# A hybrid attention and linear-recurrence layer on one core: four short gate scans, a PSUM copy shared by two engines, GpSimd's weight halves in quarters, and three memsets written earlier

## The chip, the core and the metric

The kernel runs on one core of a Trainium2 chip. The metric is the device time of one execution in microseconds (us). An instruction waits in its engine's queue behind every earlier instruction of that engine; the queues of different engines meet at semaphores.

## What is computed

One transformer layer over 16 learned meta rows and 1024 input rows of width 1024, all in float32. After an RMS norm, one projection feeds two groups of heads. Eight heads do "forgetting attention" (FoX) and four heads do a gated linear recurrence (HGRN2) in chunks; both results are joined, projected, added to the input, and followed by a SwiGLU feed-forward part. Cut to the two lines of the reference that the change touches:

```python
fox_log_f = jax.nn.log_sigmoid(ff + fox_f_bias)      # summed along the rows: s += c_i - c_j
S = jnp.exp(b_last)[..., None] * S + jnp.einsum('bhsk,bhsv->bhkv', k_dec, v_c)   # k_dec: decayed keys
```

## The kernel before

Nearly every matrix product is made of three matmuls: each float32 operand is split into a high part (a cast, on ScalarE) and a low part (source minus high part, on VectorE, or on GpSimd for some weights), and `mm3` (lines 170 to 173) issues high x high (L171), high x low (L172) and low x high (L173). These are called the dense matmuls below.

The program runs through five stages: norm, transposition and the recurrence's value projection (up to about 75 us of the trace); the HGRN heads 0 to 3 (to about 345 us); the FoX head pairs 0 to 3 (to about 575 us); the output projection; the feed-forward part (from about 675 us to the end). Stages are laid into one another: while the serial chain of one HGRN head runs on VectorE and ScalarE, TensorE fills its time with the dense matmuls of the next head's projection (`hgrn_proj`), and while attention of a pair runs, with the projection of the next pair (`fox_proj`).

Nobody writes this order out. The builder of the program takes the instructions in the order of the source, simulates them with costs of its own, and lets each engine's queue take what is ready first in that simulation. So a shorter instruction also moves other instructions, on other engines too.

What the change touches:

- `hgrn_compute` works in two units of 512 rows for each head, eight units in all. Near the end of a unit the decayed keys `kd` are transposed on TensorE (L486) into a PSUM bank, copied to `hE` by ScalarE (L488, called the key copy), and used as the stationary operand of four matmuls with the values (L491). Four VectorE instructions then update the state `S` (L498), four pairs of matmuls make the output (L495 and L496), and ScalarE and VectorE norm it before it is transposed again (L509).
- `fox_gates` sums the eight heads' gates along the rows. One scan (L349) runs over 1040 columns of 8 partitions; a mask `resetg`, written by GpSimd (L346, L348), starts the sum anew at three columns.
- `load_m` loads a 1024x128 weight. For the pairs 1 to 3, `fox_proj` has GpSimd make the low part (L140, 128x1024). There are two such weights for each pair, first for the keys and then for the queries.
- Ahead of the first pair's attention GpSimd clears two small tiles `mz` (L676) and the tail of the second head's value tile `v` (L545), in the source behind `fox_proj(0, ...)`. GpSimd also makes, for each head and each group of 256 queries, a swapped copy `QB` of the queries (L563, L564), the masked diagonal gates `dm` (L571) and a shift of the gates `nl` (L633). TensorE's score matmuls are L577 (with `QA`) and L578 (with `QB`), VectorE adds the gates to them (L583), and a score bank comes free when VectorE has read it.

Of the kernel before, what the change touches and what calls it, by code (L numbers as in the profile page):

```python
# [8 lines left out]
F32 = mybir.dt.float32  # L9
# [3 lines left out]
ALU = mybir.AluOpType  # L13
# [6 lines left out]
KT = D // P  # L20
META = 16
SEQ = 1024
L = META + SEQ
# [4 lines left out]
HEADS = 8  # L28
# [19 lines left out]
def f32(ap):  # L48
    return ap.bitcast(F32)
# [3 lines left out]
def hybrid_trunk(  # L53
# [18 lines left out]
    vec, act, pool, pe, sync = nc.vector, nc.scalar, nc.gpsimd, nc.tensor, nc.sync  # L72
# [65 lines left out]
    def split(hi, lo, src, engine=None):  # L138
        later(act.copy(hi, src))  # L139
        return later((engine or vec).tensor_sub(lo, src, f32(hi)))  # L140
# [17 lines left out]
    def load_m(c0, wsrc, engine=None):  # L158
        st = w1.tile([P, KT, P], F32, name="w_st", tag="w_st")
        sync.dma_start(out=st, in_=wsrc.rearrange("(k p) c -> p k c", p=P)[:, :, c0:c0 + P])  # L160
        hi = w1.tile([P, KT, P], F32R, name="w_hi", tag="w_hi")
        lo = w1.tile([P, KT, P], F32R, name="w_lo", tag="w_lo")
        split(hi, lo, st, engine)
        return hi, lo

    def after(ins, other):
# [164 lines left out]
    def fox_gates(z):  # L331
        az = fv.tile([P, NT + 1, HEADS], F32, name="az", bufs=1)
        act.activation(az, z, AF.Abs)
        act.activation(az, az, AF.Exp, scale=-1.0)
        act.activation(az, az, AF.Ln, bias=1.0)
        vec.tensor_scalar(z, z, 0.0, None, ALU.min)
        vec.tensor_sub(z, z, az)
        nlT = fv.tile([HEADS, L], F32, name="nlT", tag="wvh", bufs=1)
        for (dst, slots) in ((0, (NT,)), (META, (0, 1, 2, 3)), (META + 512, (4, 5, 6, 7))):
            pt = bank("tr")  # L340
            rows = META if slots[0] == NT else P
            for j, s in enumerate(slots):
                pe.transpose(pt[:HEADS, j * P:j * P + rows], z[:rows, s, :], ident[:rows, :rows])
            act.copy(nlT[:, dst:dst + rows * len(slots)], pt[:HEADS, :rows * len(slots)])
        resetg = fv.tile([HEADS, L], F32, name="resetg", tag="wvl", bufs=1)
        pool.memset(resetg, 1.0)  # L346
        for g in range(1, 4):
            pool.memset(resetg[:, META + 256 * g:META + 256 * g + 1], 0.0)  # L348
        vec.tensor_tensor_scan(nlT, resetg, nlT, 0.0, ALU.mult, ALU.add)  # L349
        sync.dma_start(out=nl_dram, in_=nlT)  # L350

    def hgrn_proj(h):
# [49 lines left out]
    def hgrn_compute(h, g, nk, qs, sgs, pm, kdm):  # L402
# [16 lines left out]
        for un in range(2):  # L419
# [65 lines left out]
            for c in range(4):  # L485
                pe.transpose(pt[:, c * P:(c + 1) * P], kd[:, c * P:(c + 1) * P], ident)  # L486
            kdT = hg.tile([P, 512], F32, name="hE", tag="hE")
            act.copy(kdT, pt)  # L488
            sb = bank("tr")
            for c in range(4):  # L490
                pe.matmul(sb[:, c * P:(c + 1) * P], lhsT=kdT[:, c * P:(c + 1) * P], rhs=hv[:, 4 * un + c, :], start=True, stop=True)  # L491
# [49 lines left out]
    def v_load(p, j, pool_):  # L541
        h = 2 * p + j
        vt = pool_.tile([P, NT + 1, P], F32R, name=f"v{j}", tag=f"v{j}", bufs=1)
        sync.dma_start(out=f32(vt[:, :NT, :]), in_=v_dram[:NT, :, h, :].rearrange("t p c -> p t c"))
        pool.memset(f32(vt[:, NT, :]), 0.0)  # L545
        for r0 in (0, 32):
            sync.dma_start(out=f32(vt[r0:r0 + META, NT, :]), in_=v_dram[NT, :META, h, :])
        return vt
# [118 lines left out]
    fx0_pool = left("fx0")  # L667
    fx0 = fx0_pool.__enter__()
    vs0, gts0 = {0: v_load(0, 0, fx0)}, [gate_load(0, j, fx0) for j in range(2)]
    b = fox_proj(0, fxk0)  # L670
    hg_pool.__exit__(None, None, None)
    fx_pool, fxk1_pool = right("fx", 2), right("fxk1")
    fx, fxk1 = fx_pool.__enter__(), fxk1_pool.__enter__()
    mzs = [fx.tile([P, 256], F32R, name=f"mz{i}", bufs=1) for i in range(2)]
    for t in mzs:
        pool.memset(f32(t), 0.0)  # L676
    for s in range(3):
        fox_compute(s, *b, *((vs0, gts0) if s == 0 else ()))
        if s == 0:
            fx0_pool.__exit__(None, None, None)  # L680
        b = fox_proj(s + 1, (fxk0, fxk1)[(s + 1) % 2])
# [522 lines left out]
```

## Time and profile before

| | us |
|---|---|
| median of 3 runs | 1296.89 (1296.81 to 1297.6) |
| the profiled execution, its own time | 1297.19 |
| span of its trace | 1295.2 |
| TensorE busy in the span | 1263.7 |
| VectorE, ScalarE, GpSimd busy | 908.6, 620.8, 126.4 |

A row of a timeline is one instruction, or several merged: start, busy time, engine, line, what it writes and reads, shapes, count; in brackets the idle time of the engine just before it and what ended it. Neighbouring instructions of one engine overlap at their ends, so the distance of two starts tells what one costs.

### The profile page before, as it was taken

The page shows a single profiled execution, that of the slowest core. Times are in us where ns is not written, and L with a number is a line of the kernel's source. Part 1 is how long each engine was busy: PE and PEld are TensorE (multiplying, and loading weights), DVE is VectorE, ACT ScalarE, POOL GpSimd, SP SyncE. Part 2 cuts the span into 40 slices and gives each one's busy share as a digit, 9 for nine tenths or more (in the row PEclk, how much of TensorE's full clock was granted, in tenths as well). Part 3 has the DMA queues.
Part 4 walks back from the last instruction along what each step waited for, and adds up shares of the span by engine and source line. Part 5 has one row for each costly group of instructions (what it writes and reads, how often), then busy time and mean ns, then how long its engine had stood idle before and what let it go on. Part 6 is the DMA issues. An engine that isn't in the chain of part 4 may idle for free.

```text
span 1295.2 us, 18497 instructions
## 1 busy us (share of the span) xinstructions
PE 1263.7 (98%) x6553; PEld 1066.5 (82%) x6553; DVE 908.6 (70%) x1889; ACT 620.8 (48%) x1334; POOL 126.4 (10%) x260
## 2 busy tenths in 40 slices
PE   8999999999899999899999999999999999999997
PEld 6888898988788888778868888888888888888886
DVE  6467666575597877796788766666666664697777
ACT  6356656464567666664453333233323333443364
POOL 1220101010334342210000000000000000000000
PEclk8999999999999999999999999999999999999999
DMA  7231212123222121533314323333332337854452
GB/s 255 74 115 45 73 42 74 58 60 115 66 92 63 59 63 47 180 111 116 127 49 139 123 82 121 122 111 106 118 122 74 114 122 265 305 194 147 122 170 82
DMA packets 135196, 146.37 MB, mean 113 GB/s; under 512 B 6984, under 2 KB 95368, under 8 KB 135104
## 3 DMA queue, kind: packets, MB, share of 16 engines
q1 hardware_dynamic: 135104, 145.19, 34.4%
q8 instruction: 52, 0.85, 0.3%
q14 instruction: 40, 0.33, 0.1%
HBM read 105.98 MB, written 39.19 MB: 112 GB/s over the span
## 4 chain that ended last, share of the span: by engine, by line
PE 81%; DVE 9%; ACT 4%; issue 2%; DMA 2%; POOL 1%; SPq 0%; DVEq 0%; ACTq 0%; POOLq 0%
PE pb L171 10%; PE pb L173 10%; PE pb L172 10%; PE dense L173 8%; PE dense L171 8%; PE dense L172 8%; PE g L171 4%; PE g L172 4%; PE g L173 4%; PE o L618 3%; PE tr L608 2%; PE g L577 1%; PE g L578 1%; DMA w_st<-in_w_in_dram 1%; PE o L172 1%
## 5 line engine op out<-in xcount | busy, mean ns | idle before, releaser
L172 PE MATMUL dense<-u_lo,w_hi 128*128 128x512 f32 (+2 forms) x384 | 141.0, 367 | 0.0
L171 PE MATMUL dense<-u_hi,w_hi 128*128 128x512 f32 (+2 forms) x384 | 140.2, 365 | 0.0
L173 PE MATMUL dense<-u_hi,w_lo 128*128 128x512 f32 (+2 forms) x384 | 139.5, 363 | 0.0
L172 PE MATMUL pb<-T_lo,bh 128*128 128x512 f32 x352 | 137.3, 390 | 0.3 <-DVE T_lo L140 0.2
L173 PE MATMUL pb<-T_hi,bl 128*128 128x512 f32 x352 | 136.9, 389 | 0.1
L171 PE MATMUL pb<-T_hi,bh 128*128 128x512 f32 x352 | 136.8, 390 | 0.2 <-ACT bh L139 0.2
L139 ACT CAST bh<-sS 128x512 fp32r<-128x512 f32 x88 | 54.3, 621 | 150.2 <-DVE sS L846 69.3
L139 ACT CAST h_hi<-h_st 128x1024 fp32r<-128x1024 f32 (+1 forms) x43 | 41.8, 972 | 82.3 <-PE o L172 37.8
L172 PEld LDWEIGHTS pb<-T_lo,bh 128*128 128x128 f32 x352 | 66.1, 188 | 15.0 <-DVE T_lo L140 1.2
L171 PEld LDWEIGHTS pb<-T_hi,bh 128*128 128x128 f32 x352 | 66.0, 188 | 14.4 <-ACT bh L139 0.6
L173 PEld LDWEIGHTS dense<-u_hi,w_lo 128*128 128x128 f32 x384 | 72.5, 189 | 6.2
L173 PEld LDWEIGHTS pb<-T_hi,bl 128*128 128x128 f32 x352 | 66.1, 188 | 14.0 <-DVE bl L140 0.4
L172 PEld LDWEIGHTS dense<-u_lo,w_hi 128*128 128x128 f32 x384 | 72.8, 190 | 5.8
L171 PEld LDWEIGHTS dense<-u_hi,w_hi 128*128 128x128 f32 x384 | 72.8, 190 | 5.7
L171 PE MATMUL pb<-w_hi,h_hi 128*128 128x512 f32 x198 | 77.0, 389 | 0.0
L172 PE MATMUL pb<-w_lo,h_hi 128*128 128x512 f32 x198 | 77.0, 389 | 0.0
L173 PE MATMUL pb<-w_hi,h_lo 128*128 128x512 f32 x198 | 77.0, 389 | 0.0
L140 DVE TENSOR_TENSOR w_lo<-w_st,w_hi 128x1024 fp32r<-128x1024 f32 (+1 forms) x41 | 49.8, 1214 | 36.8 <-ACT w_hi L139 36.6
L140 DVE TENSOR_TENSOR h_lo<-h_st,h_hi 128x1024 fp32r<-128x1024 f32 (+1 forms) x43 | 48.3, 1123 | 29.2 <-ACT h_hi L139 28.6
L139 ACT CAST w_hi<-w_st 128x1024 fp32r<-128x1024 f32 (+1 forms) x47 | 48.9, 1041 | 40.0 <-PE dense L172 17.3
L171 PE MATMUL g<-B_hi,w_hi 128*128 128x512 f32 x168 | 65.7, 391 | 0.8 <-ACT p L874 0.7
L172 PE MATMUL g<-B_lo,w_hi 128*128 128x512 f32 x168 | 65.4, 389 | 0.0
(861 smaller groups left out, 3344.1 us busy)
## 6 DMA issues: line engine op xcount, KB each, us to landing
w_st<-in_w_in_dram SPq DMA_DIRECT2D x24, 512.0 KB, 4.0
w_st<-in_w_ffn_gate_dram SPq DMA_DIRECT2D x22, 512.0 KB, 3.7
w_st<-in_w_ffn_up_dram SPq DMA_DIRECT2D x22, 512.0 KB, 3.9
B<-in_w_ffn_down_dram SPq DMA_DIRECT2D x20, 512.0 KB, 6.1
h_st<-S SPq DMA_DIRECT2D x20, 512.0 KB, 3.8
h_st<-A SPq DMA_DIRECT2D x15, 512.0 KB, 4.3
A<-g SPq DMA_DIRECT2D x22, 256.0 KB, 2.0
S<-u SPq DMA_DIRECT2D x22, 256.0 KB, 2.9
```

Source lines behind the costliest of these rows:

```text
L139: later(act.copy(hi, src))
L140: return later((engine or vec).tensor_sub(lo, src, f32(hi)))
L171: pe.matmul(o, lhsT=ah, rhs=bh, start=first, stop=False, skip_group_check=skip)
L172: pe.matmul(o, lhsT=ah, rhs=bl, start=False, stop=False, skip_group_check=skip)
L173: pe.matmul(o, lhsT=al, rhs=bh, start=False, stop=last, skip_group_check=skip)
L577: pe.matmul(sc[:, :w], lhsT=QA[:, P * i:P * (i + 1)], rhs=KS[:, c0:c0 + w], start=True, stop=False)
L578: pe.matmul(sc[:, :w], lhsT=QB[:, P * ii:P * (ii + 1)], rhs=KS[:, c0:c0 + w], start=False, stop=True)
L608: pe.transpose(pt[:, o + ii * P:o + (ii + 1) * P], Ss[ii][:, c:c + P], ident)
L618: m = pe.matmul(ob[:, q0:256], lhsT=vt[:, blk, :], rhs=r[:, q0:256], start=blk == NT, stop=blk == 2 * g + 1 and i == 3)
```

## The change

The one scan becomes four, over 272, 256, 256 and 256 columns, that read a constant 1.0 broadcast along the row; `resetg` and its memsets are gone. Of the key copy ScalarE keeps the first 256 columns and VectorE copies the other 256. GpSimd makes a weight's low part in four instructions of 128x256. The memsets of `mz` and of the second head's value tile (with that tile's load) stand ahead of `fox_proj(0, ...)` in the source.

```diff
-        split(hi, lo, st, engine)
+        if engine is None:
+            split(hi, lo, st)
+            return hi, lo
+        act.copy(hi, st)
+        for k in range(0, KT, 2):
+            engine.tensor_sub(lo[:, k:k + 2], st[:, k:k + 2], f32(hi[:, k:k + 2]))
...
-        resetg = fv.tile([HEADS, L], F32, name="resetg", tag="wvl", bufs=1)
-        pool.memset(resetg, 1.0)
-        for g in range(1, 4):
-            pool.memset(resetg[:, META + 256 * g:META + 256 * g + 1], 0.0)
-        vec.tensor_tensor_scan(nlT, resetg, nlT, 0.0, ALU.mult, ALU.add)
+        for a, b in ((0, META + 256), (META + 256, META + 512), (META + 512, META + 768), (META + 768, L)):
+            vec.tensor_tensor_scan(nlT[:, a:b], reset4[:HEADS, 1:2].to_broadcast([HEADS, b - a]), nlT[:, a:b], 0.0, ALU.mult, ALU.add)
...
-            act.copy(kdT, pt)
+            act.copy(kdT[:, :256], pt[:, :256])
+            vec.tensor_copy(kdT[:, 256:], pt[:, 256:])
...
-    b = fox_proj(0, fxk0)
...
         pool.memset(f32(t), 0.0)
+    vs0[1] = v_load(0, 1, fx)
+    b = fox_proj(0, fxk0)
```

Lines of the changed kernel stand 2 to 5 further down than before: L486 is L488 there, L491 is L494, L495 and L496 are L498 and L499, the low parts of GpSimd are L168, the dense matmuls L176 to L178.

TensorE's queue in the first unit, from the transposition of the decayed keys (`tr` out of `ident` and `hX`) to the first output matmuls, before:

```order
L486 MATMUL tr<-ident,hX 128x128 x4
L448 MATMUL g<-hX 128x128 x2
L172 MATMUL dense<-u_lo,w_hi 128x384
L173 MATMUL dense<-u_hi,w_lo 128x384
L171 MATMUL dense<-u_hi,w_hi 128x384
L491 MATMUL tr<-hv,hE 128x128 x4
L495 MATMUL o<-hv,AT 128x128
L496 MATMUL o<-S,hY 128x128
```

The same place after the change:

```order
L488 MATMUL tr<-ident,hX 128x128 x4
L450 MATMUL g<-hX 128x128 x2
L177 MATMUL dense<-u_lo,w_hi 128x384
L494 MATMUL tr<-hv,hE 128x128 x2
L498 MATMUL o<-hv,AT 128x128
L494 MATMUL tr<-hv,hE 128x128 x2
L499 MATMUL o<-S,hY 128x128
L498 MATMUL o<-hv,AT 128x128
```

Two dense matmuls that stood ahead of the four value matmuls now stand behind them, and the four are two pairs with an output matmul between.

TensorE's queue in the last unit, from the last dense matmuls of the first pair's keys (384 wide) on; `g` out of `KS` and `QA` is a score matmul of the first pair, and the 512-wide dense matmuls are that pair's second query projection, 24 in all. Before:

```order
L173 MATMUL dense<-u_hi,w_lo 128x384
L171 MATMUL dense<-u_hi,w_hi 128x512
L448 MATMUL g<-hX 128x128 x2
L491 MATMUL tr<-hv,hE 128x128 x4
L577 MATMUL g<-KS,QA 128x256
L172 MATMUL dense<-u_lo,w_hi 128x512
L173 MATMUL dense<-u_hi,w_lo 128x512
L495 MATMUL o<-hv,AT 128x128
```

After:

```order
L176 MATMUL dense<-u_hi,w_hi 128x384
L177 MATMUL dense<-u_lo,w_hi 128x384
L450 MATMUL g<-hX 128x128 x2
L494 MATMUL tr<-hv,hE 128x128 x2
L580 MATMUL g<-KS,QA 128x256
L494 MATMUL tr<-hv,hE 128x128 x2
L498 MATMUL o<-hv,AT 128x128
L499 MATMUL o<-S,hY 128x128
```

The three 512-wide matmuls of this piece have moved behind the output matmuls. Further on, 14 of the 24 stand behind the unit's first output transposition (L509, now L512) where 9 stood before, and three 272-wide dense matmuls stand behind the first two matmuls that read `QB`, where all 24 of their kind stood ahead of them.

GpSimd's queue from the low parts of the second pair's two weights (`w_lo`) to the first pair's gates (`nl`), with the numbers of the buffers. Before:

```order
L140 TENSOR_TENSOR w_lo_4411<-w_st_4408,w_hi_4410 128x1024
L140 TENSOR_TENSOR w_lo_4417<-w_st_4414,w_hi_4416 128x1024
L676 MEMSET mz0_3661 128x256
L676 MEMSET mz1_3662 128x256
L545 MEMSET v1_3665 128x128
L563 COPY QB_3672<-QA0_3580 64x256
L564 COPY QB_3672<-QA0_3580 64x256
L571 AFFINE_SELECT dm_3676<-nl0_3572 128x128
```

After (the first line is the whole first weight and the second three quarters of the second):

```order
L168 TENSOR_TENSOR w_lo_4417<-w_st_4414,w_hi_4416 128x256 x4
L168 TENSOR_TENSOR w_lo_4426<-w_st_4423,w_hi_4425 128x256 x3
L678 MEMSET mz0_3593 128x256
L678 MEMSET mz1_3594 128x256
L548 MEMSET v1_3597 128x128
L566 COPY QB_3678<-QA0_3602 64x256
L567 COPY QB_3678<-QA0_3602 64x256
...
L168 TENSOR_TENSOR w_lo_4426<-w_st_4423,w_hi_4425 128x256
L548 MEMSET v0_4490 128x128
L636 TENSOR_SCALAR nl0_3578<-nl0_3578,tg0_3580 128x272
L574 AFFINE_SELECT dm_3733<-nl1_3582 128x128
```

The memsets keep their place behind the weights; one quarter has moved behind the first six `QB` copies, ahead of the gates. At the next two pairs both weights are done, as before, ahead of one `dm` and the `QB` copies that follow it.

## Rows read from the trace of the kernel before

**Rows 1.** The page: busy us, share of the span and instructions of each engine.

```profile
PE 1263.7 (98%) x6553; PEld 1066.5 (82%) x6553; DVE 908.6 (70%) x1889; ACT 620.8 (48%) x1334; POOL 126.4 (10%) x260
```

**Rows 2.** The waits of TensorE, summed by who waited for whom: us in total, times, longest.

```profile
PE tr L491 <- ACT hE L488: 2.5, 8, 0.4
PE g L578 <- POOL QB L564: 2.0, 1, 2.0
...
PE g L577 <- DVE rr L590: 1.0, 1, 1.0
```

**Rows 3.** The timeline of TensorE and VectorE in the first unit.

```profile
114.02 1.16 PE L491 MATMUL tr<-hv,hE 128*128 128x128 f32 x8 [0.34 <-ACT hE L488]
...
115.22 1.64 DVE L498 SCALAR_TENSOR_TENSOR S<-S,hP,tr 128x128 f32<-128x128 f32 x4 [1.22 <-PE tr L491]
```

**Rows 4.** The timeline of ScalarE and VectorE in the second unit, and TensorE's wait behind it.

```profile
135.09 0.59 ACT L488 COPY hE<-tr 128x512 f32<-128x512 f32 x1
...
135.09 0.69 DVE L482 TENSOR_TENSOR hY<-hP,hg_q 128x512 f32<-128x512 f32 x1 [0.96 <-ACT hP L480]
...
136.92 1.64 DVE L498 SCALAR_TENSOR_TENSOR S<-S,hP,tr 128x128 f32<-128x128 f32 x4
138.59 1.22 DVE L425 TENSOR_TENSOR_SCAN hP<-reset,hg_g 128x512 f32<-128x512 f32 x1
...
142.25 0.33 PE L509 MATMUL tr<-ident,hE 128*128 128x128 f32 x1 [0.55 <-ACT hE L506]
```

**Rows 5.** The timeline around the gate scan: a 256-wide cast out of PSUM by ScalarE, a 256-wide read of PSUM by VectorE, the scan and what follows it on VectorE.

```profile
302.64 0.37 ACT L326 CAST vt<-dense 128x256 fp32r<-128x256 f32 x1 [3.21 <-DMA v_dram<-vt]
...
303.05 0.42 DVE L327 TENSOR_TENSOR vt<-dense,vt 128x256 fp32r<-128x256 f32 x1 [3.08 <-ACT vt L326]
...
309.69 2.31 DVE L349 TENSOR_TENSOR_SCAN nlT<-resetg,nlT 8x1040 f32<-8x1040 f32 x1 [0.66 <-ACT nlT L344]
311.93 0.39 DVE L472 TENSOR_TENSOR hP<-hP 128x256 f32<-128x256 f32 x1
```

**Rows 6.** TensorE in the last two units: its waits, and the first and the last of the nine 512-wide dense matmuls behind the first L509.

```profile
313.56 0.33 PE L486 MATMUL tr<-ident,hX 128*128 128x128 f32 x1 [0.98 <-ACT hX L400]
...
335.02 0.33 PE L486 MATMUL tr<-ident,hX 128*128 128x128 f32 x1 [0.22 <-ACT hX L400]
...
337.46 1.16 PE L491 MATMUL tr<-hv,hE 128*128 128x128 f32 x8 [0.38 <-ACT hE L488]
...
344.15 0.33 PE L509 MATMUL tr<-ident,hE 128*128 128x128 f32 x1 [0.26 <-ACT hE L506]
344.24 0.48 PE L171 MATMUL dense<-u_hi,w_hi 128*128 128x512 f32 x1
...
346.33 0.39 PE L172 MATMUL dense<-u_lo,w_hi 128*128 128x512 f32 x1
346.56 0.39 PE L173 MATMUL dense<-u_hi,w_lo 128*128 128x512 f32 x1
```

**Rows 7.** From the second weight's high part (ScalarE) through GpSimd's queue to the two waits of TensorE and the one of VectorE.

```profile
346.76 1.05 ACT L139 CAST w_hi<-w_st 128x1024 fp32r<-128x1024 f32 x1 [1.88 <-PE dense L172]
...
347.88 2.39 POOL L140 TENSOR_TENSOR w_lo<-w_st,w_hi 128x1024 fp32r<-128x1024 f32 x1 [6.71 <-ACT w_hi L139]
350.21 0.57 POOL L676 MEMSET mz<- 128x256 f32 x2
...
350.99 0.39 POOL L563 CAST QB<-QA 64x256 fp32r<-64x256 f32 x1
...
354.96 0.54 POOL L571 TENSOR_SCALAR_AFFINE_SELECT dm<-nl 128x128 f32<-128x128 f32 x2
...
351.89 0.51 PE L578 MATMUL g<-KS,QB 128*128 128x256 f32 x2 [1.98 <-POOL QB L564]
...
355.79 0.42 PE L577 MATMUL g<-KS,QA 128*128 128x400 f32 x1 [0.96 <-DVE rr L590]
...
355.28 0.35 DVE L583 CUSTOM_DVE_ANT_0 S__3731<-g,dm,mx 128x128 f32<-128x128 f32 x1 [1.26 <-POOL dm L571]
```

**Rows 8.** GpSimd's groups, shapes kept apart: busy us and mean ns of one instruction.

```profile
L633 POOL TENSOR_SCALAR nl<-nl,tg 128x784 f32<-128x784 f32 x8 | 7.8, 974 | 2.2 <-DVE mx L583 1.9
...
L633 POOL TENSOR_SCALAR nl<-nl,tg 128x272 f32<-128x272 f32 x8 | 3.9, 492 | 10.1 <-DVE mx L583 7.3 <-issue 2.7
```

**Rows 9.** The next pair's second weight, the `QB` copy behind it, and the first score matmul that reads a fresh `QB` there.

```profile
409.81 2.39 POOL L140 TENSOR_TENSOR w_lo<-w_st,w_hi 128x1024 fp32r<-128x1024 f32 x1 [6.42 <-ACT w_hi L139]
...
412.51 0.39 POOL L564 CAST QB<-QA 64x256 fp32r<-64x256 f32 x1
...
414.65 0.34 PE L578 MATMUL g<-KS,QB 128*128 128x384 f32 x1
```

**Rows 10.** Stretches of 2 us: length, busy time and count of TensorE, its weight loads, VectorE, ScalarE and GpSimd, granted clock, share and rate of the DMA engines.

```profile
350.00:352.00 2.00, 0.11 (x1) 0.11 (x2) 0.36 (x1) 0.32 (x1) 1.80 (x7) 1.00 0.01 3
...
522.00:524.00 2.00, 0.49 (x2) 0.30 (x2) 1.97 (x6) 1.95 (x4) 1.21 (x2) 1.00 1.08 291
524.00:526.00 2.00, 1.25 (x4) 0.90 (x5) 1.94 (x3) 1.60 (x4) 0.96 (x2) 0.82 1.00 218
526.00:528.00 2.00, 2.00 (x6) 1.54 (x5) 1.53 (x6) 0.00 (x0) 0.26 (x1) 0.50 0.92 336
528.00:530.00 2.00, 2.00 (x10) 1.78 (x10) 1.32 (x7) 0.00 (x0) 0.97 (x3) 0.83 0.98 381
```

## The prediction

> **What bounds the kernel now.** I read the page's busy times first, then TensorE's waits summed by who was waited for, then the timelines around every line that the change touches, and last GpSimd's groups and 2 us stretches with the granted clock. TensorE is busy 1263.7 of 1295.2 us [rows 1], so 31.5 us of idle time is all that can be won without taking matmuls away, and the change takes none away. Of that idle time it can reach three pieces: the eight waits of L491 for the key copy, 2.5 us in all; the first wait for a `QB`, 2.0; and a wait of 1.0 behind VectorE that is really GpSimd's `dm` [rows 2]. The last two are one place, 347 to 356, where GpSimd's queue is the path. So the question in each part is whether a shorter or longer step ends a wait of TensorE, or whether another step is late just behind it.
>
> **The key copy in halves.** In the first unit L491 waits 0.34 for the copy, and its eight matmuls end at 115.18, where VectorE's state update L498 starts after a wait of 1.22 [rows 3]. ScalarE's copy of 512 columns takes 0.59 [rows 4]; a 256-wide cast out of PSUM took 0.37, and a 256-wide VectorE read of PSUM 0.42 [rows 5]. So both halves, side by side, end 0.22 earlier at best, and eight units give 8 x 0.22 = 1.8 us as the largest gain. VectorE's own busy time grows by 8 x 0.42 = 3.4 us.
>
> What is late next: in the first unit two 384-wide dense matmuls, which filled the time of the copy, now stand behind L491. A 512-wide one costs 0.23, the distance of two starts [rows 6], so 384 columns cost 0.17 each, and the wait becomes 0.34 - 0.22 + 2 x 0.17 = 0.46. The two matmuls are not lost, they are done later. But L498 needs all four value products, and the second pair now stands behind an output matmul of about 0.22: 0.58 + 0.22 + 0.58 = 1.38 in the place of 1.16 [rows 3]. The group starts 0.22 earlier and lasts 0.22 longer, so `S` comes at the same time. In the second unit VectorE's queue is full from L498 through the scan L425, and TensorE waits 0.55 at L509 for what comes out of it [rows 4]; an earlier copy makes that wait longer by what it saves. VectorE's 0.42 lies in its own wait for the transposition's products, idle anyway before L498 (1.22 in the first unit). If that cover is gone, the units whose end is set by VectorE's chain pay it: three times 0.42 = +1.3. I take 0, between -1.8 and +1.3, because the two units that I followed both give back what they win.
>
> **Four scans.** A scan over 512 columns takes 1.22 [rows 4], over 1040 columns 2.31 [rows 5]: 1.09 for 528 columns, 2.06 ns each, and 0.16 fixed. Four over the same 1040 columns are 2.14 + 4 x 0.16 = 2.80, +0.49; bounds 0 (the fixed part overlaps) and +0.5. It lies on a path: VectorE goes from the scan straight to the chain of the seventh unit (L472, 311.93) [rows 5], behind which TensorE waits 0.98 at 313.56 [rows 6]. That wait grows by 0.49. What comes later and isn't fed by it gives some back: the waits of 0.22 at 335.02 and 0.38 at 337.46 [rows 6] shrink when TensorE comes later to them. I let +0.2 through to the end of the last unit and count it there. The mask's memsets on GpSimd are on no path, and their going is worth 0.
>
> [...]
>
> **The last unit and GpSimd's queue.** Here the order matters more than the durations. In the last unit two of the three 512-wide matmuls of the listed piece no longer stand between L491 and the first output matmuls: -0.46. With the copy's -0.22 and the +0.2 from the scans the unit's first L509 (344.15) comes about 0.45 to 0.5 earlier. Nine 512-wide dense matmuls stood behind it, the last at 346.56 [rows 6]; now there are 14, 5 x 0.23 = 1.15 more. The next weight's high part on ScalarE (346.76) starts when the last but one of these has ended, and GpSimd's low part (347.88, 2.39 us) when the high part has [rows 7]. So both start 0.65 to 0.7 later.
>
> Then the quarters. A quarter is not in the trace. The low end is 2.39 / 4 = 0.60. GpSimd's `nl` gives the fixed part: 0.974 for 784 columns and 0.492 for 272 [rows 8], 0.94 ns for each and 0.24 fixed; the whole weight bears that once and a quarter as well, so a quarter is (2.39 - 0.24) / 4 + 0.24 = 0.78, the high end. I take 0.75, near the high end, because `nl` is the nearest row of the same engine and a similar size. Three quarters are then 2.25, 0.14 less than the whole. The fourth no longer stands ahead of the first `QB` copies but ahead of `dm`.
>
> [...]
>
> So the first `QB` comes 0.65 - 0.14 = 0.5 later, and TensorE's wait at 351.89 grows by about that. Three 272-wide dense matmuls (3 x 0.12 = 0.37) that TensorE did ahead of this wait it now does behind it, in the next wait, at no cost. `dm` (354.96) comes 0.5 + 0.75 = 1.25 later; VectorE waits 1.26 for it at L583 (355.28) and TensorE behind that at L577 (355.79) [rows 7]. The delay at the end of this place is the later of the two, not their sum: **+1.25**. Bounds: +0.45 (the scans cost nothing, a quarter takes 0.60), and +1.7 (the scans' 0.49 goes through whole, a quarter takes 0.78).
>
> **Pairs 2 and 3.** Both weights still stand ahead of one `dm` and the `QB` copies there, so these come 4 x 0.75 - 2.39 = 0.6 later. The copy at 412.51 is one of two of 0.39; both would be done by 413.3, and its first reader stands at 414.65 without a wait [rows 9]: 1.3 us of slack hide the 0.6. I take +0.1 for each of the two places, for readers that are nearer than the one shown, +0.2; bounds 0 and +1.4 (0.6 and what queues behind it).
>
> **The moved memsets** keep their place in GpSimd's queue behind the weights, where they take 0.78, from 350.21 to the `QB` copy at 350.99 [rows 7], and win nothing: 0.
>
> **Sum.** 0 + 1.25 + 0.2 = +1.45 on the profiled execution's 1297.19 is 1298.64; that execution is 0.30 above the median of the runs shown, so 1298.3.
>
> **The rivals.** *Faster.* [...] 0.10.
>
> *Slower by a clock fall.* [...] 0.18.
>
> *Nothing changes.* The halves win 0.22 in some units (together about -1.2), GpSimd's place loses about that, and the moved memsets do nothing, since the queue keeps them: 1296.9 to 1297.2. For it: terms of both signs and similar size. Against it: the key copy's waits are short of followers in few units only. 0.22.
>
> **How the numbers follow.** My forecast, the sum, gets 0.50. About 0.2% (2.6 us) is what a measurement of this kernel can tell from no change: 1294.3 to 1299.5. The forecast lies inside it, with a tail above it where the key copy's +1.3 or the pairs' +1.4 comes: 0.07 of its 0.50. So slower is 0.18 + 0.07 = 0.25, faster 0.10, and the same 0.43 + 0.22 = 0.65. The range goes from 1295.2, the sum with the low ends of the key copy and of GpSimd's place (1298.3 - 1.8 - 0.8 = 1295.7) and 0.5 towards the faster rival, to 1300.6, the clock rival with the pairs' excess; it leaves out the faster rival and the sum of all high ends.
>
> **What would show it.** Right: L491's waits fall to about half, and L498 starts no earlier; a quarter takes 0.70 to 0.78; the four scans together 2.7 to 2.8; the first wait for `QB` is 2.4 to 2.6 and the wait for `dm` behind it over 1.5; the granted clock at 350 stays 1.00. Wrong: TensorE's idle time falls by over 1 us in the HGRN stage, or a quarter takes 0.60, or the second wait at 355 doesn't grow though `dm` is later, or the clock at 350 or at 524 is another than before.

## The result, and the profile after

| | before | after |
|---|---|---|
| median, lowest, highest of 18 runs each, us | 1296.16 (1294.38 to 1297.81) | 1298.82 (1297.01 to 1299.90) |
| the profiled execution, its own time | 1297.19 | 1299.88 |
| span of its trace | 1295.2 | 1298.2 |

The ratio is 1.0018 (95% interval 1.0012 to 1.0025): the changed kernel is slower by 2.7 us in the medians, 1.6 to 3.2 by the interval. The forecast was 1298.3, +1.4 on its own base. The time lies in the range and the sign is right, but the loss is nearly twice the sum, and most of it stands in another place.

TensorE's row on the page, and its waits summed by who was waited for (us, times, longest), which answer to [rows 1, 2]:

```profile
PE 1263.3 (97%) x6553; PEld 1066.1 (82%) x6553; DVE 913.1 (70%) x1900; ACT 620.2 (48%) x1334; POOL 125.7 (10%) x274
```

```profile
PE tr L512 <- ACT hE L509: 2.6, 4, 0.9
...
PE g L581 <- POOL QB L567: 2.1, 1, 2.1
PE tr L494 <- ACT hE L490: 1.7, 5, 0.5
...
PE o L499 <- DVE S L501: 1.0, 4, 0.3
```

The reader is to see that the waits for the key copy fell, from 2.5 us in eight to 1.7 in five, and that two others have come up in their place. TensorE now waits 1.0 us in four at the output matmuls that read the state S, where the list of the kernel before has no wait. At the output transposition (L512) it waits 2.6 us in four, where the kernel before waited twice, 0.55 and 0.26 [rows 4, 6]. TensorE has as much work as before, 1263.3 against 1263.7 [rows 1].

Where the time went can be read from the starts of a few TensorE instructions that both kernels issue. The first four are the state products of the heads 0 to 3 (L415, `tr` out of `kdmT`, one at the start of each head), then the first key transposition of the seventh unit (L486), the first matmul that reads a `QB`, the first 400-wide score matmul, and the 272-wide score matmul behind the wait at 523. Between them lie the heads 0, 1 and 2, the end of the gate scan, the last two units with GpSimd's place, and the pairs 0 to 2. The numbers in the first two rows are the distances of these starts. The last two units lie in the column "to the first QB", together with GpSimd's weights.

| us | head 0 | head 1 | head 2 | to unit 7 | to the first QB | to the 400-wide | pairs 0 to 2 |
|---|---|---|---|---|---|---|---|
| before: starts 104.93, 170.34, 237.84, 309.91, 313.56, 351.89, 355.79, 522.81 | 65.41 | 67.50 | 72.07 | 3.65 | 38.33 | 3.90 | 167.02 |
| after: 104.96, 170.77, 239.07, 311.94, 315.19, 353.84, 358.44, 525.80 | 65.81 | 68.30 | 72.87 | 3.25 | 38.65 | 4.60 | 167.36 |
| after less before | +0.40 | +0.80 | +0.80 | -0.40 | +0.32 | +0.70 | +0.34 |

So +2.0 of the +2.96 arises in the heads 0 to 2, where only the key copy differs and TensorE does the same matmuls. The next three columns do not hold the same matmuls in both kernels: one dense matmul of 512 columns (0.23 us) has moved out of "to unit 7", and three of 272 columns (0.37) have moved into "to the 400-wide". Only their sum compares like with like: from the scans to the end of GpSimd's place the change costs -0.40 + 0.32 + 0.70 = +0.62.

**The key copy.** VectorE's timeline in the fourth unit (the second of head 1) of the kernel before; this place is in no group:

```profile
198.10 1.22 DVE L140 TENSOR_TENSOR w_lo<-w_st,w_hi 128x1024 fp32r<-128x1024 f32 x1
199.24 1.22 DVE L425 TENSOR_TENSOR_SCAN hP<-reset,hg_g 128x512 f32<-128x512 f32 x1
200.40 0.35 DVE L498 SCALAR_TENSOR_TENSOR S<-S,hP,tr 128x128 f32<-128x128 f32 x1
...
203.12 0.34 DVE L498 SCALAR_TENSOR_TENSOR S<-S,hP,tr 128x128 f32<-128x128 f32 x1
```

The same unit after the change, VectorE, ScalarE and TensorE (L490 and L491 are the two halves of the copy, L494 the value matmuls):

```profile
198.59 1.22 DVE L140 TENSOR_TENSOR w_lo<-w_st,w_hi 128x1024 fp32r<-128x1024 f32 x1
199.06 0.37 ACT L490 COPY hE<-tr 128x256 f32<-128x256 f32 x1
199.73 0.42 DVE L491 COPY hE<-tr 128x256 f32<-128x256 f32 x1
200.87 0.62 DVE L371 SCALAR_TENSOR_TENSOR hg_n<-gx,lnomlb,gs 128x384 f32<-128x384 f32 x1 [0.72 <-ACT gs L367]
...
201.94 0.35 DVE L501 SCALAR_TENSOR_TENSOR S<-S,hP,tr 128x128 f32<-128x128 f32 x1
...
203.12 1.21 DVE L427 TENSOR_TENSOR_SCAN hP<-reset,hg_g 128x512 f32<-128x512 f32 x1
...
205.09 0.34 DVE L501 SCALAR_TENSOR_TENSOR S<-S,hP,tr 128x128 f32<-128x128 f32 x1
```

```profile
199.49 0.71 PE L494 MATMUL tr<-hv,hE 128*128 128x128 f32 x4 [0.32 <-ACT hE L490]
...
200.74 0.48 PE L178 MATMUL dense<-u_hi,w_lo 128*128 128x512 f32 x1
201.06 0.40 PE L176 MATMUL dense<-u_hi,w_hi 128*128 128x512 f32 x1
201.29 0.61 PE L494 MATMUL tr<-hv,hE 128*128 128x128 f32 x4
...
209.34 0.33 PE L512 MATMUL tr<-ident,hE 128*128 128x128 f32 x1 [0.57 <-ACT hE L509]
```

ScalarE's half starts at 199.06 and takes 0.37, as forecast. VectorE's half takes the forecast 0.42, but it starts 0.67 later, behind the low part `w_lo` of the next head's weight (198.59, 1.22 us). Not all of the 0.67 is the low part's: in each of the eight units VectorE's half starts only after ScalarE's has ended, 0.40 to 0.73 behind its start, and in the first and the seventh VectorE is idle before it, 0.23 and 0.59, until ScalarE's half is done. TensorE's own queue then adds to it: two dense matmuls stand ahead of the second pair of value matmuls, which start 1.1 us after the half is there (201.29 against 200.15). The builder's simulation, it seems, had the half later still; that is not shown. A scan of 1.2 us stands between the state updates as well. The first S starts 201.94 against 200.40, the last 205.09 against 203.12. Seen from the unit's first key transposition (196.66 before, 197.14 after) that is 1.06 and 1.49 us later, and TensorE waits 0.57 at the output transposition, where the view of the kernel before shows no wait in this unit.

The second unit, which the prediction followed, loses too (changed kernel; the rows before are in [rows 4]):

```profile
136.72 0.61 PE L494 MATMUL tr<-hv,hE 128*128 128x128 f32 x4
137.37 1.63 DVE L501 SCALAR_TENSOR_TENSOR S<-S,hP,tr 128x128 f32<-128x128 f32 x4 [0.50 <-PE tr L494]
...
142.70 0.33 PE L512 MATMUL tr<-ident,hE 128*128 128x128 f32 x1 [0.55 <-ACT hE L509]
```

Counted from the unit's first key transposition (133.42 before, 133.57 after), the first S starts 0.30 later, behind the second pair of value matmuls, and the output transposition 0.29 later, with the same wait of 0.55.

**The scans.** One merged row, which answers to the scan in [rows 5]:

```profile
311.18 2.46 DVE L351 TENSOR_TENSOR_SCAN nlT<-reset,nlT 8x272 f32<-8x272 f32 x4
```

The four take 2.46 together, 0.15 more than the one. And the view shows no wait ahead of them: the one scan had waited 0.66 for ScalarE to bring the last columns [rows 5], while the first of the four starts at 311.18, 0.44 before ScalarE's last copies into that tile end (311.62).

**GpSimd's place.** The rows that answer to [rows 7, 8]: GpSimd's queue, the two waits of TensorE, VectorE's wait for the gates, and the group of all quarters (busy us, mean ns):

```profile
350.11 2.12 POOL L168 TENSOR_TENSOR w_lo<-w_st,w_hi 128x256 fp32r<-128x256 f32 x3 [5.07 <-ACT w_hi L166]
...
356.30 0.73 POOL L168 TENSOR_TENSOR w_lo<-w_st,w_hi 128x256 fp32r<-128x256 f32 x1
...
353.84 0.51 PE L581 MATMUL g<-KS,QB 128*128 128x256 f32 x2 [2.07 <-POOL QB L567]
...
358.44 0.42 PE L580 MATMUL g<-KS,QA 128*128 128x400 f32 x1 [1.29 <-DVE rr L593]
...
357.94 0.35 DVE L586 CUSTOM_DVE_ANT_0 S__3737<-g,dm,mx 128x128 f32<-128x128 f32 x1 [1.60 <-POOL dm L574]
```

```profile
L168 POOL TENSOR_TENSOR w_lo<-w_st,w_hi 128x256 fp32r<-128x256 f32 x24 | 17.1, 737 | 56.1 <-PE dense L178 35.2 <-ACT w_hi L166 20.8
```

GpSimd's first low part, the norm's first and third step on VectorE in the last unit, and TensorE's wait behind them, after; the last row is the first of these steps before:

```profile
342.19 2.85 POOL L168 TENSOR_TENSOR w_lo<-w_st,w_hi 128x256 fp32r<-128x256 f32 x4 [35.23 <-PE dense L178]
342.96 0.69 DVE L108 TENSOR_SCALAR rs_v<-oss 128x4 f32<-128x4 f32 x1 [1.36 <-ACT hE L506]
344.47 0.59 DVE L112 TENSOR_TENSOR rs_t<-rs_t,rs_v 128x4 f32<-128x4 f32 x1
345.91 0.33 PE L512 MATMUL tr<-ident,hE 128*128 128x128 f32 x1 [0.91 <-ACT hE L509]
...
342.26 0.17 DVE L108 TENSOR_SCALAR rs_v<-oss 128x4 f32<-128x4 f32 x1 [1.30 <-ACT hE L503]
```

The two steps, 128x4 each, take 0.69 and 0.59 where they took 0.17 and 0.16 before, and each ends 0.02 us after a quarter on GpSimd (343.63 and 345.04). Whether the quarters hold them up was not tested.

The granted clock around GpSimd's place and around the later fall, in stretches of 2 us with the columns of [rows 10]:

```profile
352.00:354.00 2.00, 0.16 (x1) 0.16 (x2) 0.59 (x1) 0.00 (x0) 1.80 (x7) 1.00 0.01 3
...
356.00:358.00 2.00, 1.15 (x10) 0.76 (x8) 0.24 (x3) 0.45 (x2) 1.91 (x6) 1.00 0.51 152
526.00:528.00 2.00, 0.66 (x4) 0.27 (x3) 1.97 (x4) 1.95 (x5) 1.88 (x3) 0.85 1.08 290
528.00:530.00 2.00, 2.00 (x6) 1.49 (x5) 1.94 (x5) 0.70 (x2) 0.02 (x1) 0.50 0.76 233
530.00:532.00 2.00, 2.00 (x9) 1.68 (x8) 1.14 (x6) 0.00 (x0) 0.70 (x1) 0.79 0.80 307
```

### The profile page after: what moved, and what is told of

Its sections match the earlier page's. It is cut to its first block, busy times and chain, and to the rows that moved or that the text cites. A ratio compares the mean times of both kernels' runs of the same rounds, so it can differ in the third digit from the quotient of the medians.

```text
span 1298.2 us, 18521 instructions
## 1 busy us (share of the span) xinstructions
PE 1263.3 (97%) x6553; PEld 1066.1 (82%) x6553; DVE 913.1 (70%) x1900; ACT 620.2 (48%) x1334; POOL 125.7 (10%) x274
## 4 chain that ended last, share of the span: by engine, by line
PE 80%; DVE 10%; ACT 5%; DMA 2%; issue 2%; POOL 1%; SPq 0%; DVEq 0%; ACTq 0%; POOLq 0%
PE pb L176 10%; PE pb L178 10%; PE pb L177 10%; PE dense L178 8%; PE dense L176 8%; PE dense L177 8%; PE g L176 4%; PE g L178 4%; PE g L177 4%; PE o L621 2%; PE tr L611 2%; PE g L580 1%; PE g L581 1%; DMA w_st<-in_w_out_dram 1%; PE o L178 1%
## 5 line engine op out<-in xcount | busy, mean ns | idle before, releaser
L176 PE MATMUL dense<-u_hi,w_hi 128*128 128x512 f32 (+2 forms) x384 | 140.3, 365 | 0.0
L178 PE MATMUL dense<-u_hi,w_lo 128*128 128x512 f32 (+2 forms) x384 | 139.5, 363 | 0.0
L178 PE MATMUL pb<-T_hi,bl 128*128 128x512 f32 x352 | 136.9, 389 | 0.1
L176 PE MATMUL pb<-T_hi,bh 128*128 128x512 f32 x352 | 136.8, 390 | 0.1
L176 PEld LDWEIGHTS pb<-T_hi,bh 128*128 128x128 f32 x352 | 66.0, 188 | 14.5 <-ACT bh L139 0.6
L178 PEld LDWEIGHTS dense<-u_hi,w_lo 128*128 128x128 f32 x384 | 72.7, 189 | 6.1
L178 PEld LDWEIGHTS pb<-T_hi,bl 128*128 128x128 f32 x352 | 66.1, 188 | 14.0 <-DVE bl L140 0.4
L176 PEld LDWEIGHTS dense<-u_hi,w_hi 128*128 128x128 f32 x384 | 72.8, 189 | 5.8
L176 PE MATMUL pb<-w_hi,h_hi 128*128 128x512 f32 x198 | 77.0, 389 | 0.0
L178 PE MATMUL pb<-w_hi,h_lo 128*128 128x512 f32 x198 | 77.0, 389 | 0.0
L176 PE MATMUL g<-B_hi,w_hi 128*128 128x512 f32 x168 | 65.7, 391 | 0.8 <-ACT p L878 0.7
L178 PE MATMUL g<-B_hi,w_lo 128*128 128x512 f32 x168 | 65.4, 389 | 0.0
```

The lines of the kernel that those rows point to most:

```text
L176: pe.matmul(o, lhsT=ah, rhs=bh, start=first, stop=False, skip_group_check=skip)
L178: pe.matmul(o, lhsT=al, rhs=bh, start=False, stop=last, skip_group_check=skip)
```

## The experiments

The median of 11 runs of each kernel (18 for the changed kernel) stands beside that of the kernel before, run together with it; ratios are to the kernel before. The last four columns are worked out as in the table above, from one profiled execution of each: kernel less before. They reach from 105 to 523 us of the trace, and what lies ahead of that and behind it differs from trace to trace as well (770.8 to 774.4 us behind). So the medians tell what a kernel costs, and the columns where; the two differ most in experiment 10, by 1.0 us.

| kernel | median, us (before beside it) | ratio (95% interval) | heads 0, 1, 2 | to unit 7 | to QB, to 400-wide | pairs 0 to 2 |
|---|---|---|---|---|---|---|
| changed kernel | 1298.82 (1296.16) | 1.0018 (1.0012 to 1.0025) | +0.40, +0.80, +0.80 | -0.40 | +0.32, +0.70 | +0.34 |
| 1 whole copy | 1297.29 (1296.54) | 1.0009 (1.0000 to 1.0017) | 0.00, +0.04, 0.00 | -0.40 | -0.90, -0.14 | +2.99 |
| 2 halves only | 1298.75 (1296.54) | 1.0018 (1.0009 to 1.0027) | +0.42, +0.78, +0.81 | -0.01 | -0.04, +0.01 | -0.12 |
| 3 quarters only | 1297.07 (1296.54) | 1.0004 (0.9995 to 1.0013) | -0.05, +0.06, -0.02 | -0.01 | +0.41, 0.00 | +0.35 |
| 4 scans only | 1296.67 (1296.54) | 1.0000 (0.9992 to 1.0009) | +0.02, +0.06, -0.02 | -0.41 | +0.33, +0.01 | -0.15 |
| 5 halves, both ScalarE | 1297.23 (1296.27) | 1.0008 (0.9999 to 1.0016) | +0.32, +0.34, +0.28 | 0.00 | -0.20, +0.54 | +0.18 |
| 6 memsets only | 1296.29 (1296.27) | 0.9999 (0.9990 to 1.0008) | +0.02, +0.04, -0.01 | -0.01 | +0.03, +0.02 | 0.00 |
| 7 whole copy on VectorE | 1296.70 (1296.27) | 1.0000 (0.9991 to 1.0009) | -0.62, +1.07, +1.00 | 0.00 | -0.64, +0.02 | +0.33 |
| 8 half ahead | 1295.33 (1296.27) | 0.9994 (0.9985 to 1.0003) | -0.01, -0.02, -0.29 | -0.01 | -0.05, 0.00 | -0.11 |
| 9 states first | 1297.50 (1296.33) | 1.0007 (0.9999 to 1.0016) | +0.03, +0.91, +0.57 | -0.01 | -0.02, +0.50 | -0.28 |
| 10 changed, half ahead | 1296.25 (1296.33) | 0.9998 (0.9990 to 1.0007) | -0.12, +0.04, -0.23 | -0.40 | +0.35, +0.71 | +0.60 |
| 11 half ahead, low part on VectorE | 1294.22 (1296.33) | 0.9983 (0.9974 to 0.9992) | -0.07, 0.00, -0.24 | -0.01 | -2.25, -0.81 | +2.15 |
| 12 low part on VectorE | 1294.09 (1296.33) | 0.9984 (0.9976 to 0.9993) | -0.04, +0.07, 0.00 | -0.01 | -1.98, -0.89 | +1.36 |

### The parts one by one

**1. Whole copy.** The changed kernel with the key copy as it was:

```diff
-            act.copy(kdT[:, :256], pt[:, :256])
-            vec.tensor_copy(kdT[:, 256:], pt[:, 256:])
+            act.copy(kdT, pt)
```

> The changed kernel with one part undone: ScalarE copies all 512 columns of the decayed keys again. Theory A (the late half): VectorE's half stands in its queue behind other work, behind a low part of 1.22 us in the second units of two heads, so the second pair of value matmuls, the state S and all behind it come later, and TensorE waits at the matmuls that read S and at the output transposition; about 1.5 of the +2.7 us come from there, so this kernel stands at +1.0 to +1.3 to the kernel before and those waits are gone. Theory B (the prediction's sum: the key copy gives back what it wins, GpSimd's quarters and the longer queue behind the last unit make the loss): it stands at +2.3 to +2.7, as the changed kernel.

+0.75 us in the medians (interval 0.0 to 2.2), where the changed kernel stands at +2.66: theory A's side, a little below its +1.0. The heads 0 to 2 are back at the times of before. That GpSimd's place is 1.0 shorter here and the pairs 3.0 longer was not expected by either. 0.46 of the 3.0 are two dense matmuls of 512 columns that moved there, and TensorE waits for VectorE (`mx`) six times, 3.6 us in all, where the kernel before waited once, 1.5; why the order differs was not followed further.

**2. Halves only.** The kernel before with the opposite edit of 1.

> The kernel before with the halved key copy alone. Theory A: +1.3 to +1.8 us, with waits of some 0.2 to 0.6 at the matmuls that read S and at the output transposition in the second units, which the kernel before does not have. Theory B: 0 (within 0.5), since the waits for the copy fall and others grow by as much.

+2.2 us (interval 1.2 to 3.5), above theory A's range, with the changed kernel's waits in the same places but for the 0.91 of the last unit, and the same +0.4, +0.8, +0.8 in the heads. The part alone makes most of the loss. Theory B's 0 has fallen.

**3. Quarters only.** The new `load_m` of the change in the kernel before.

> The kernel before with GpSimd's low parts in quarters alone. Theory B: +0.8 to +1.3 us, since the fourth quarter of 0.73 now stands ahead of the gates of the first pair. Theory A: +0.3 to +0.5, for the wait behind the gates grew by 0.33 only, from 0.96 to 1.29, and the wait for the swapped queries by 0.1.

+0.5 us with an interval that holds 0: theory A's value. The trace has +0.41 at the first `QB` and nothing up to the 400-wide matmul: alone, all four quarters stand ahead of the `QB` copies. So theory B's place (the fourth quarter ahead of the gates) arises only with the other parts.

**4. Scans only.** The four scans of the change in the kernel before.

> The kernel before with the four scans alone. Theory B: +0.2 to +0.5 us, what four fixed parts of 0.16 cost on the path into the seventh unit. Theory A: 0 to +0.2, as TensorE's wait in that unit did not grow (0.98 before, 0.81 in the changed kernel).

0.1 us. Unit 7 begins 0.41 earlier, with one dense matmul (0.23) less ahead of it, and the next two units, which have that matmul, give it back (+0.33). Theory A's 0 to 0.2 holds in the trace, for a reason that it did not have: in the changed kernel's trace the first scan no longer waits for the last columns (0.66 before). The interval (-1.0 to +1.2) would hold theory B's value as well.

**6. Memsets only.** The two moves of the change in the source around `fox_proj(0, ...)`, nothing else.

> The kernel before with the memsets and the load of the second head's values written earlier, nothing else. Both theories: 0, within 0.3 us, for the memsets keep their place in GpSimd's queue. A third, that the shifted load changes what comes late in the first pair: +0.5 or more.

0.0 us, and no stretch differs by more than 0.04. The four parts measured alone sum to 2.2 + 0.5 + 0.1 + 0.0 = 2.8, the whole is 2.7; each part's interval is about 1.1 us to either side.

### What of the halved copy costs the time

**5. Both halves on ScalarE.**

```diff
-            act.copy(kdT, pt)
+            act.copy(kdT[:, :256], pt[:, :256])
+            act.copy(kdT[:, 256:], pt[:, 256:])
```

> The kernel before with the key copy in two halves, both on ScalarE. Theory A1 (VectorE's queue: the half stands there behind other work): VectorE has nothing to do with this copy, so 0, between -0.5 and +0.4 us. Theory A2 (cutting the copy is the fault, since each half pays a fixed part and the value products come in two pieces): +1 to +2.2, as the halves shared with VectorE.

+1.0 us (interval -0.1 to +2.1), between the two: 0.3 in each head. VectorE's queue has no part of this copy, so theory A1 is not all of it. The order of the value matmuls is again four in a row here, and the last S of the fourth unit starts 0.32 earlier in the unit than before (6.14 us after its first key transposition). Yet the waits at the output transposition come back with 0.75 in the heads 1 and 2. What is late is the norm behind it:

```profile
202.22 0.63 ACT L380 ACTIVATE gs<-gs 128x512 f32<-128x512 f32 x1
202.76 0.26 ACT L504 ACTIVATE hE<-o 128x128 f32<-128x128 f32 x1
...
204.68 1.22 DVE L425 TENSOR_TENSOR_SCAN hP<-reset,hg_g 128x512 f32<-128x512 f32 x1
```

ScalarE squares the outputs (L504) at 202.76, behind steps of the projection, though the last output matmul ended at 201.95. VectorE takes 2.75 us from the norm's first small step to its last (203.91 to 206.66), with a scan and two steps of 0.69 between them, against 2.26 before. So here, too, the order in the queues makes the wait, though VectorE has no part of the copy. Less than half of the loss of 2.

**7. Whole copy on VectorE.**

```diff
-            act.copy(kdT, pt)
+            vec.tensor_copy(kdT, pt)
```

> The kernel before with the whole key copy on VectorE, all 512 columns: the suspected cost doubled. Theory A1 (the place in the queue decides): in the order of this kernel no low part of 1.22 us stands ahead of the copy, so +0.5 to +1.8 us, not above the halves' +2.2. Theory A3 (VectorE's added busy time decides, which is 0.42 for each half and about 0.7 for a whole copy in each of eight units): 1.7 times the halves' loss, +3.0 to +4.5.

0.4 us in the medians, a ratio of 1.0000 (interval -1.2 to +1.2). Theory A3 (VectorE's added busy time) has fallen: with more work on VectorE than in 2 the kernel is 1.8 us faster than 2. Theory A1's +0.5 to +1.8 begins just above the median, and the interval reaches into it: heads 1 and 2 lose 1.0 each, since steps of the projection and a scan stand ahead of the state updates, while head 0 and the stretch to the first `QB` win 0.6 each.

**8. Half ahead.** The halves of 2, and one order held: the two parts of the next head's third weight, the high one on ScalarE and the low one on VectorE, may not stand ahead of VectorE's half.

```diff
+            first['copy'] = vec.tensor_copy(kdT[:, 256:], pt[:, 256:])
...
+            if tag == "hg_s" and "copy" in first:
+                hold.append(first["copy"])
             w = load_m(c + h * P, w_in[0])
+            hold.clear()
```

> The halves alone again, with one thing held: the low part of the next head's third weight is put behind VectorE's half of the key copy, which brings the state updates back to the order of the kernel before as well. Theory A1: the waits at the matmuls that read S and at the output transposition in the second units of the second and third head go, 1.3 us and more, so 0 to +0.8 against the kernel before, in the place of +2.2. Theories A2 and A3 (the cut itself, or VectorE's added time): it stays at +1.5 to +2.2.

-0.9 us (interval -1.9 to +0.4), 3 us below 2. The +1.5 to +2.2 of theories A2 and A3 has fallen, and the gain is more than A1 gave it, though the interval reaches into A1's 0 to +0.8. ScalarE and VectorE in the fourth unit of this kernel:

```profile
198.80 1.04 ACT L140 CAST w_hi<-w_st 128x1024 fp32r<-128x1024 f32 x1
...
198.67 0.42 DVE L493 COPY hE<-tr 128x256 f32<-128x256 f32 x1
...
199.89 0.35 DVE L503 SCALAR_TENSOR_TENSOR S<-S,hP,tr 128x128 f32<-128x128 f32 x1 [0.34 <-PE tr L496]
200.16 1.22 DVE L141 TENSOR_TENSOR w_lo<-w_st,w_hi 128x1024 fp32r<-128x1024 f32 x1
...
202.86 0.33 DVE L503 SCALAR_TENSOR_TENSOR S<-S,hP,tr 128x128 f32<-128x128 f32 x1
```

The copy stands first, VectorE even waits 0.34 for the products, the low part runs between two state updates, and the last update starts 6.65 us after the unit's first key transposition (196.21), against 7.95 in the changed kernel and 6.46 before. The hold names two instructions: the high part's cast on ScalarE, which stood at 191.09 in the changed kernel, has moved here too. The builder then also put the state updates back between the projection's steps, and the second value pair, which comes at 199.14, right behind the half. The experiment shows that the order around the halved copy is the cause, not the cut or VectorE's added time; which of the moved instructions does it, it does not show.

VectorE took its queue in order there: in the fourth unit of the changed kernel ScalarE's half was done at 199.43 (199.06 + 0.37), and VectorE's started at 199.73, behind the low part, whose 1.22 us began at 198.59.

**9. States first.** As 8, with the projection's last two steps held behind the first state update and the next head's first scan behind the last.

```diff
+            if un == 0 and (1, 3) in first:
+                after(scan, first[1, 3])
...
+            if (1, 0) in first and c0 == FULL[2][0]:
+                after(nki, first[1, 0])
+                after(gci, first[1, 0])
```

> As the kernel with the half held ahead of the low part, with more of the order held: the projection's two steps on the last 384 columns behind the first state update of the second unit, the next head's first scan behind the last one. Theory A1 in its narrow form (the low part ahead of the copy is all of the loss): within 0.5 us of the kernel with the half ahead, -0.9. In its wide form (every VectorE step that the builder puts between the copy and the state updates counts): 0.5 to 1.0 us below that kernel.

A miss for both forms: +1.2 us against the kernel before (interval -0.1 to +2.1), 2.1 above 8. VectorE and TensorE in the fourth unit:

```profile
199.75 1.22 DVE L141 TENSOR_TENSOR w_lo<-w_st,w_hi 128x1024 fp32r<-128x1024 f32 x1 [0.73 <-ACT w_hi L140]
...
204.78 1.22 DVE L432 TENSOR_TENSOR_SCAN hP<-reset,hg_g 128x512 f32<-128x512 f32 x1
205.91 0.15 DVE L108 TENSOR_SCALAR rs_v<-oss 128x4 f32<-128x4 f32 x1
205.96 1.22 DVE L432 TENSOR_TENSOR_SCAN hP<-reset,hg_g 128x512 f32<-128x512 f32 x1
207.09 0.14 DVE L111 TENSOR_TENSOR rs_t<-rs_y 128x4 f32<-128x4 f32 x1
...
209.32 0.59 PE L519 MATMUL tr<-ident,hE 128*128 128x128 f32 x2 [1.09 <-ACT hE L516]
```

The state updates are in time (the last starts 6.74 after the unit's first key transposition, 196.40), but the held scan now stands in front of the norm's small steps (`rs_v`, `rs_t`), the second scan between them, and TensorE waits 1.09 at the output transposition. So what has to come early is the whole chain from the copy to the norm; here two long steps near its end brought a wait of 1.09.

**10. Changed kernel, half ahead.** The change with the hold of 8.

> The changed kernel, all of it, with the one hold added: the low part of the next head's third weight behind VectorE's half of the key copy. Theory A1: it loses the halves' +2.2 and gains 0.9 as the halves alone did, so 2.7 - 3.1 = -0.4, between -0.9 and +0.6 against the kernel before. If the parts of the change do not add up (rival: quarters and the longer queue behind the last unit cost +1.25 of their own, as the prediction had it), +0.5 to +1.3.

-0.1 us (interval -1.3 to +0.9), in the range of A1. The heads are as in 8, the scan's 0.4 and the +0.35 and +0.71 behind it as in the changed kernel. With the order held the change costs nothing that can be told from 0, and it brings nothing. The rival is not out: behind the heads the columns of this one trace sum to +1.26.

### GpSimd's queue

**12. Low part on VectorE**, and **11** with the hold of 8 as well. The low part of the second pair's query weight is made whole by VectorE:

```diff
-        wk, wq = (load_m(c + p * P, w_in[0], pool if p else None) for c in (C_FK, C_FQ))
+        wk, wq = (load_m(c + p * P, w_in[0], pool if p > 1 or p and c == C_FK else None) for c in (C_FK, C_FQ))
```

> The kernel before with that low part on VectorE alone. Same two readings without the halves: -1.5 to -2.9 us if GpSimd's queue is the path there, 0 to -0.8 if another chain ends as late.

> Held halves, and the low part of the second pair's query weight made by VectorE, whole, in the place of GpSimd (1.2 us in the place of 2.39, and off the queue of the swapped queries and the gates). If GpSimd's queue is what TensorE waits for at 350 and 355 (1.98 and 0.96), 1.5 to 2.9 us are won on top of the held halves' -0.9: -2.4 to -3.8. If those waits are followed by others that end as late (the softmax on VectorE and ScalarE), 0 to 0.8 on top.

-2.2 us (interval -3.1 to -0.9) alone, and -2.1 with the halves held: both beat both kernels. GpSimd, VectorE and TensorE in 12:

```profile
341.63 0.39 POOL L563 CAST QB<-QA 64x256 fp32r<-64x256 f32 x1
...
347.75 1.23 DVE L140 TENSOR_TENSOR w_lo<-w_st,w_hi 128x1024 fp32r<-128x1024 f32 x1 [1.72 <-ACT w_hi L139]
...
349.65 0.40 PE L578 MATMUL g<-KS,QB 128*128 128x256 f32 x2
...
365.10 0.33 PE L608 MATMUL tr<-ident,S__3946 128*128 128x128 f32 x1 [0.49 <-DVE mz L599]
```

The first `QB` copy runs at 341.63 in the place of 350.99, the low part takes 1.23 on VectorE, which had waited 1.72 for the high part, and both waits, 1.98 and 0.96 [rows 7], are gone: 2.87 us won up to the 400-wide matmul, in line with the expectation's first reading. The pairs give 1.36 of it back in new waits behind VectorE, as the one of 0.49 at 365.10. With the halves held they give back 2.15, and what 8 won is lost there; the expectation of -2.4 to -3.8 for 11 was missed.

## Why the prediction was right, and where it was not

The sign, the range and the likeliest case hold: the measured 0.18% lies just inside the 0.2% that was called the same, though its interval reaches 0.25%. But the sum had 0 + 1.25 + 0.2 = +1.45, the runs have +2.66, and the three terms measured in the trace are +2.0, +0.62 and +0.34. One term was missed by 2.0 and another was 0.6 too large, so the right time is in part luck: two errors of opposite sign, and a range wide enough for the rest.

**The key copy, taken at 0, measured +2.2 in experiment 2, +2.0 of it in the heads.** This is the step that failed. The durations were right (0.37 and 0.42), the wait in the first unit was right (0.48, 0.46 forecast), and there S came at the same time (3.38 us after the first key transposition, 3.37 before). The step that failed is the choice of 0 "because the two units that I followed both give back what they win", and the sentence that VectorE's 0.42 lies in its own wait. Already the second of these units loses 0.3. In the second units of the heads 1 and 2 the half stood behind the low part on VectorE and the second value pair behind dense matmuls on TensorE, and steps of the projection that had stood between the state updates moved ahead of them. The bound of +1.3, three units at 0.42, was too narrow as well: what such a step costs is the wait in the queue and what the builder then reorders, not its own length. In the heads 1 and 2 TensorE's idle time grew by 0.66 and 0.69 of the 0.80 each. In head 0 it did not grow, and why that head takes 0.40 longer stays open. The halves also did not run side by side: in the first unit VectorE's ended 0.82 after ScalarE's had begun (0.40 + 0.42), where the whole copy takes 0.59 [rows 4].

**Four scans, taken at +0.49 for the seventh unit and +0.2 behind it, measured 0.1.** The row with the answer was in the list: the one scan's 0.66 of waiting for ScalarE's copies [rows 5]. The pieces overlap with these copies, and their own cost is 0.15, not 0.49; TensorE's wait at the seventh unit is 0.81 where it was 0.98 and 1.47 was forecast. Each further scan cost 0.05 (0.15 / 3), where 0.16 had been taken.

**GpSimd's place, taken at +1.25, measured +0.62**, from the start of the fourth head to the 400-wide matmul (46.50 against 45.88). A quarter took 0.737 busy (0.75 taken), the wait for the gates was 1.60 (over 1.5 forecast) and the clock 1.00. What was wrong is how late the queue starts. The text ahead of the prediction counts 14 dense matmuls of 512 columns behind the last unit's first output transposition in the changed kernel; the trace has 11, so 2 x 0.23 = 0.46 are added to the 9, not 1.15. And that transposition came 0.27 earlier, not 0.45 to 0.5 (33.97 us after the start of the head against 34.24), although the output matmuls ahead of it were done 0.47 earlier in the unit: the norm's two slow steps, above, stand between. So the second low part began 0.20 later and not 0.65 to 0.7; three quarters, 0.70 apart, saved 0.27; and the first `QB` came 0.08 earlier, not 0.5 later. Its wait grew by 0.09 only. The fourth quarter's 0.70 is what remains: 0.70 - 0.08 = 0.62. From the whole (2.39) and the quarter (0.737), each of the 768 further columns took (2390 - 737) / 768 = 2.15 ns.

**Pairs 2 and 3** (+0.2) and **the memsets** (0) were about right: +0.34 for the pairs 0 to 2, and 0.0 us in experiment 6.

**The rivals.** The range's upper end, 1300.6, is built on a clock fall at GpSimd's place. No run shows that term: in the 2 us from 352 TensorE was busy 0.16 and in those from 356 1.15, with full work between them (2.00), and the clock stayed at 1.00. The later fall is as before (0.85, 0.50, 0.79 from 526 to 532, and 0.82, 0.50, 0.83 from 524 to 530 [rows 10]), so the faster rival won nothing there. "Nothing changes" rested on the copy's gain, which is there in waits and not in time.

What stays open: how the loss of the halved copy divides between the low part ahead of it, the builder's other moves on VectorE and TensorE, and the cut itself (experiment 5 gives up to 1.0 of 2.2 to a cut without VectorE, in which the norm came late behind other steps, and experiment 8 gives none); and why the pairs give back 3.0 in experiment 1 and 2.15 in experiment 11.

## What to carry to other kernels

A step that is handed to a second engine is only as early as that engine's queue lets it be, as the half here, behind a low part of 1.22 us: read what stands ahead of it in every unit of the loop, not in the first two, and in the queue of the engine that uses its result; and hold the order (here of the two parts of one weight, 3 us between experiments 2 and 8) where a long step of the next stage gets in front of a chain. A wait for the last columns ahead of a long instruction, as the scan's 0.66 here, is what cutting the instruction can win. Where two stretches of two kernels are compared, count the matmuls in each first. And where two engines can make the same data, give it to the one whose queue is not being waited for: the low part moved off GpSimd's queue won 2.2 us, more than any cut.

## What was not expected of the hardware

Four scans over 1040 columns took 2.46 against 2.31 for one, 0.05 us for each further instruction, where the lengths of two scans had given 0.16. A GpSimd low part of 128x1024 took 2.85 in four quarters in a row against 2.39 whole (a quarter is busy 0.737, but starts 0.70 after the one before), and VectorE made a low part of that size in 1.23. Two 128x4 steps on VectorE took 0.69 and 0.59 in the place of 0.17 and 0.16 and ended with a quarter on GpSimd; a cause is not shown.
